# A two-layer encoder trunk on one core: two paddings resized, and the second half of the first activation block turned into a job of the first step

## The chip, the cores and the metric

The kernel runs on one core of one Trainium2 chip. The metric is the device time of one execution in microseconds. The kernel before was timed three times: 2141.28, 2142.65 and 2142.89 us, median 2142.65 us. A fourth execution was taken with the hardware profiler; its time was 2141.81 us.

## What is computed

The input x has 256 positions and 2048 features in float32. Two layers run one after the other, each a mixer followed by a SwiGLU feed-forward block, and a last RMSNorm ends the trunk. What matters here is the first matrix product, ab_in, which follows the first norm, and that every large product is a matmul of 128 x 128 by 128 x 512:

```
for layer in range(2):
    h = rms_norm(x, mix_norm[layer])
    x = x + (mixer_ab(h) if layer == 0 else mixer_c(h))
    h = rms_norm(x, ffn_norm[layer])
    x = x + (silu(h @ w_gate) * (h @ w_up)) @ w_down
out = rms_norm(x, final_norm)
```

## The kernel before, in words

**Products.** Each float32 product is made of three fp32r matmuls (function `three`, L480): the operands are split in a high part and a low rest (activations `xh`, `xl`; weights `whi`, `wlo`), and high x high (L481), high x low (L482) and low x high (L483) are added into one PSUM bank. The activations, transposed, are the stationary operand (loaded by a weight load); the weights are the moving operand of 512 columns. In the views a matmul is written `b<-moving,stationary`.

**Stages and steps.** Eight stages follow each other: ab_in (12 blocks of 512 output columns), ab_out (4), up0 (11), down0 (4), c_in (8), c_out (4), up1 (11), down1 (4). A block is cut into steps. A plain step (`kind` std) takes 4 of the 128-row pieces of the weights and makes 24 matmuls, 12 in each half; up0 and up1 are mixed stages whose steps combine operands to save products (24 or 21 matmuls a step, 183 a block; some take their moving operand from `ha` and `la` instead of `whi` and `wlo`). In all there are 376 steps and 8826 such matmuls.

**Operands.** The stationary operand is xh/xl in ab_in and c_in (pools x_a and x_next), cath/catl in ab_out (pool cat), ush/usl in c_out (pool us), fh/fl in the mixed stages (pool forms), jh/jl in down0 and down1 (pool split). Pools on the left side of SBUF are stacked in the order const, wpool, resid, small, and then the ones opened and closed during the work (x_a, mix_a, mixw, forms, x_next, split); cat, us, ffn and mix_c are stacked from the right side. Tiles take multiples of 32 bytes. Three tiles that nobody reads, CONST_PAD, SMALL_PAD and RIGHT_PAD, only shift what follows. In the program of the kernel before the bytes at which the tiles begin in a partition are:

```
stage .. mhalf (const)   16512, 17024, 17536, 17920, 18432   mhalf has 8 bytes
gain0 (const)            19392     = mhalf + 32 + 928
raw, whi, wlo (wpool)    19456 .. 68608                      all multiples of 1024
x0 .. x3 (resid)         76800 .. 89088                      all multiples of 1024
ssq (small)              93440     = 93184 + 256
xh0 (x_a), tt (mixw)     96320     = 94 x 1024 + 64
ha, la (mixw)            104512, 110656                      multiples of 1024 + 64
fh0, fl0, fh1, fl1       120896, 123968, 127040, 130112      multiples of 1024 + 64
fh2, fl2, fh3, fl3       133184, 136768, 140352, 143424      fl2 a multiple of 512 + 64
fh4, fl4 .. fh6, fl6     146496, 150080 .. 159808, 163392    fl4, fl6 likewise
jh, jl (split)           137280 .. 161856                    multiples of 1024 + 64
cath0 .. catl3, us       195584 .. 224256                    all multiples of 1024
```

**Order of work.** `load(t)` issues the weights of step t on SP's queue (three `raw` buffers), `prep(t)` splits them: two casts on ScalarE (L259, `whi`) and two subtractions on VectorE (L265, `wlo`), into one of two buffers, which is free when the step that used it is done. At the end of step t, `end_step` (L523) loads step t + 4 and prepares step t + 2. Other work is put in a heap by `later(dt, fn)` with a due time counted in half steps; `jobs_due(2t)` runs what is due at the beginning of step t and `jobs_due(2t + 1)` between its halves; equal due times keep the order in which they were put in. `x_transposes(st, n)` makes the operands xh and xl of 512 columns of x: per half 4 transposes on TensorE into a PSUM bank (banks 4 and 5 in turn, L127), two activations on ScalarE (L409), two operations on VectorE (L413). Until the job due at 9 the order on ScalarE and VectorE is that of the program (`manual_schedule`, L618 to L621, closed by L656); TensorE's order is chosen by the compiler's scheduler.

**The start.** On SP's queue, in order: columns 0 to 255 of x0 (the first 512 features of x), two pieces of the weights of step 0, columns 256 to 511 of x0, the rest of step 0's weights, x1, weights of step 1, x2, weights of step 2, x3, and later the weights of step 3. L642 to L657 then give the order of the preparation, which the change edits. The jobs put in are: x_transposes 2 due at 1, x_transposes 3 due at 3, squares of x0 to x3 due at 3 to 6, transpose_vectors due at 4, finish_norm due at 7.

Of the kernel before, what the change touches and what calls it, by code (L numbers as in the profile page):

```python
# [9 lines left out]
F32 = mybir.dt.float32  # L10
# [6 lines left out]
P = 128  # L17
# [17 lines left out]

CONST_PAD = 928
SMALL_PAD = 256
RIGHT_PAD = 992  # L40

RC = 4
# [3 lines left out]
PREP_AHEAD = 2  # L46
# [29 lines left out]
def trunk_kernel(  # L76
# [18 lines left out]
    nc = tc.nc  # L95

    const = ctx.enter_context(tc.tile_pool(name="const", bufs=1))
    wpool = ctx.enter_context(tc.tile_pool(name="wpool", bufs=1))
    resid = ctx.enter_context(tc.tile_pool(name="resid", bufs=1))
    small = ctx.enter_context(tc.tile_pool(name="small", bufs=2))  # L100
    small.tile([P, SMALL_PAD // 4], F32, name="small_pad", bufs=1)
    right = ctx.enter_context(tc.tile_pool(name="right", bufs=1, side="right"))
# [81 lines left out]
    def load(t):  # L184
        if t >= len(steps) or t in raws:
            return
        s = steps[t]
        r = wpool.tile([P, RC, NB], F32, tag="raw", name="raw", bufs=RAW_BUFS)
        raws[t] = r

        def part(dst, w, c0, k, n):
            nc.sync.dma_start(
                dst, w[k * P : (k + n) * P, c0 : c0 + NB].rearrange("(k p) n -> p k n", p=P)
            )

        if s.kind != "std":
            for side, (w, c0) in enumerate(s.src):
                part(r[:, side::2, :], w, c0, s.k0, 2)
            return
        (w, c0), = s.src  # L200
        if t:
            part(r, w, c0, s.k0, RC)
        else:
            for k in range(2):
                part(r[:, k : k + 1, :], w, c0, k, 1)
            return lambda: part(r[:, 2:4, :], w, c0, 2, 2)
# [5 lines left out]
    def prep_a_hi(t):  # L212

        if t in parts_a:
            return
        hi = mixw[0].tile([P, 3, NB], F32R, tag="ha", name="ha")
        nc.scalar.copy(hi, raws[t][:, 1:4, :])
        parts_a[t] = (hi, None)

    def prep_a_lo(t):  # L220
        hi, lo = parts_a[t]
        if lo is None:
            lo = mixw[0].tile([P, 3, NB], F32R, tag="la", name="la")
            nc.vector.tensor_tensor(
                out=lo, in0=raws[t][:, 1:4, :], in1=hi.bitcast(F32), op=ALU.subtract
            )
            parts_a[t] = (hi, lo)

    def combine_first(t):

        if t in sums:
            return
        load(t)
        sums[t] = tt = mixw[0].tile([P, RC, NB], F32, tag="tt", name="tt")
        r = raws[t]
        nc.vector.tensor_tensor(
            out=tt[:, 0:2, :], in0=r[:, 0:3:2, :], in1=r[:, 1::-1, :], op=ALU.subtract
        )

    def combine_rest(t):  # L240

        if t in whole:
            return
        combine_first(t)
        whole.add(t)
        r, tt = raws[t], sums[t]
        for i in range(2):
            nc.vector.tensor_tensor(
                out=tt[:, 2 + i, :], in0=r[:, 2 + i, :], in1=tt[:, 2 * i, :], op=ALU.subtract
            )  # L250

    def cast_half(t, h):
        if t not in parts:
            load(t)
            hi = wpool.tile([P, RC, NB], F32R, tag="whi", name="whi", bufs=W_BUFS)
            lo = wpool.tile([P, RC, NB], F32R, tag="wlo", name="wlo", bufs=W_BUFS)
            parts[t] = (hi, lo)
        r = sums[t] if steps[t].kind == "S" else raws[t]
        nc.scalar.copy(parts[t][0][:, HALF[h], :], r[:, HALF[h], :])  # L259

    def low_part(t, h):
        hi, lo = parts[t]
        r = sums[t] if steps[t].kind == "S" else raws[t]
        sl = HALF[h]
        nc.vector.tensor_tensor(  # L265
            out=lo[:, sl, :], in0=r[:, sl, :], in1=hi[:, sl, :].bitcast(F32), op=ALU.subtract
        )

    def prep(t):

        if t >= len(steps) or t in parts:
            return
        load(t)
        if steps[t].kind == "S":
            combine_first(t)
            combine_rest(t)
        for h in "01":
            cast_half(t, h)
            low_part(t, h)
        if steps[t].kind == "S":  # L280
            prep_a_hi(t)
            prep_a_lo(t)
        if steps[t].pi in operand:
            operand[steps[t].pi].split(steps[t].k0 // RC)
# [11 lines left out]
    def later(dt, fn):  # L296
        heapq.heappush(jobs, (now[0] + dt, seq[0], fn))
        seq[0] += 1
# [15 lines left out]
    ident = const.tile([P, P], F32, name="ident")  # L314
    make_identity(nc, ident)
    mhalf = const.tile([P, M], F32, name="mhalf")
    const.tile([P, CONST_PAD // 4], F32, name="const_pad")
    nc.gpsimd.memset(mhalf, -0.5)
    vec_at = {}
# [61 lines left out]
    def transpose_pair(src, c0):  # L381

        pt = tp_bank()
        for j in range(2):
            for m in range(M):
                nc.tensor.transpose(  # L386
                    out=pt[:, j * S + m * P : j * S + (m + 1) * P],
                    in_=src[:, m, c0 + j * P : c0 + (j + 1) * P],
                    identity=ident,
                )  # L390
        return pt
# [4 lines left out]
    def x_transposes(st, n, halves=(0, 1)):  # L396
        if st.mixed:
            for i in (2 * n, 2 * n + 1):
                x_forms(st, xs[n], i)
            return  # L400
        if n not in st.hi:
            st.hi[n] = st.pool[0].tile([P, 4, S], F32R, tag=f"xh{n}", name=f"xh{n}")
            st.lo[n] = st.pool[0].tile([P, 4, S], F32R, tag=f"xl{n}", name=f"xl{n}")
        hi, lo = st.hi[n], st.lo[n]
        for half in halves:
            pt = transpose_pair(xs[n], half * 2 * P)
            cols = [4 * n + half * 2 + j for j in range(2)]
            for j, c in enumerate(cols):
                nc.scalar.activation(  # L409
                    hi[:, c % 4, :], pt[:, j * S : (j + 1) * S], AF.Copy, scale=gain_col(st, c)  # L410
                )
            for j, c in enumerate(cols):
                nc.vector.scalar_tensor_tensor(  # L413
                    out=lo[:, c % 4, :], in0=pt[:, j * S : (j + 1) * S], scalar=gain_col(st, c),
                    in1=hi[:, c % 4, :].bitcast(F32), op0=ALU.mult, op1=ALU.subtract,
                )

    def x_forms(st, src, i):

        pt = tp_bank()  # L420
        c0 = (2 * i % 4) * P
        for j, (kk, m) in enumerate(((0, 1), (0, 0), (1, 0), (1, 1))):
            nc.tensor.transpose(  # L423
                out=pt[:, j * P : (j + 1) * P], in_=src[:, m, c0 + kk * P : c0 + (kk + 1) * P],
                identity=ident,
            )
        f = st.pool[0].tile([P, 8, P], F32, tag="f", name="f")
        for kk in range(2):
            nc.scalar.activation(
                f[:, 2 * kk : 2 * kk + 2, :].rearrange("p a b -> p (a b)"),  # L430
                pt[:, kk * S : (kk + 1) * S], AF.Copy, scale=gain_col(st, 2 * i + kk),
            )

        def combine(dst, a, b, op):
            nc.vector.tensor_tensor(out=f[:, dst, :], in0=f[:, a, :], in1=f[:, b, :], op=op)

        if MIX[i] == "S":
            combine(4, 0, 3, ALU.add)
            combine(5, 1, 0, ALU.subtract)
            combine(6, 4, 1, ALU.subtract)  # L440
            combine(7, 2, 6, ALU.subtract)
            n, used = S_FORMS, f[:, 1:8, :]
        else:
            combine(slice(4, 6), slice(1, 3), slice(0, 4, 3), ALU.subtract)
            n, used = N_FORMS, f[:, 0:6, :]
        hi = st.pool[0].tile([P, n, P], F32R, tag=f"fh{i}", name=f"fh{i}")
        lo = st.pool[0].tile([P, n, P], F32R, tag=f"fl{i}", name=f"fl{i}")
        split(hi, lo, used)
        st.hi[i], st.lo[i] = hi, lo
# [73 lines left out]
    def end_step(t, evac):  # L523
        now[0] = 2 * t + 2
        del parts[t]
        cur[0] += 1
        evac()
        load(t + LOAD_AHEAD)
        prep(t + PREP_AHEAD)

    BANKS = {1: 6, 6: 7, 7: 5, 2: 0, 5: 1, 3: 2, 4: 3}

# [90 lines left out]
    st = new_norm("mix0")  # L623
# [15 lines left out]
    def first_split(a, b):  # L639
        split(hi0[:, a:b, :], lo0[:, a:b, :], raws[0][:, a:b, :])  # L640

    x_transposes(st, 0, (0,))  # L642
    first_split(0, 1)
    first_split(1, 2)
    x_transposes(st, 0, (1,))
    first_split(2, 4)
    x_transposes(st, 1)
    parts[0] = (hi0, lo0)
    load(3)
    prep(1)  # L650
    for n in (2, 3):
        later(2 * n - 3, lambda n=n: x_transposes(st, n))
    for n in range(4):
# [504 lines left out]
```

## Time and profile before

| what | value |
|---|---|
| median of the three runs | 2142.65 us |
| the profiled execution | 2141.81 us, of which its span 2140.0 us |
| TensorE busy (matmul) | 2121.4 us, 99% of the span, 9356 instructions |
| VectorE busy | 1500.9 us, 70% |
| ScalarE busy | 1119.6 us, 52% |
| transfers | 404.80 MB, mean 189 GB/s |

The span runs from the first to the last instruction of the program; the rest of the execution's time lies around it. A busy TensorE is not TensorE at its peak: matmuls are pipelined, each is recorded from its start to its modelled end, and two of them overlap in the record. What a stream of matmuls costs is the time from one start to the next.

### The profile page before, as it was taken

How to read it: one execution, taken by the hardware profiler on the slowest of the kernel's cores; microseconds unless marked ns; L12 is line 12 of the kernel's file. 1: busy time of each engine (PE TensorE's matmuls, PEld its weight loads, DVE VectorE, ACT ScalarE, POOL GpSimd, SP SyncE). 2: the span in 40 equal slices, each digit the busy share in tenths (PEclk: the TensorE clock that was granted, in tenths of full speed). 3: DMA queues.
4: the chain of work that ended last, by engine and by line, in shares of the span. 5: the costliest groups of instructions: out<-in, count | busy, mean ns of one | idle time of the engine just before them, and what ended most of it. 6: DMA issues, size and time to landing. Idle time of an engine off the chain costs nothing.

```text
span 2140.0 us, 24018 instructions
## 1 busy us (share of the span) xinstructions
PE 2121.4 (99%) x9356; PEld 1715.4 (80%) x9356; DVE 1500.9 (70%) x1591; ACT 1119.6 (52%) x1327; POOL 17.8 (1%) x37
## 2 busy tenths in 40 slices
PE   8999999999999999999999999999999999999998
PEld 7888888888888888788888888888888888878886
DVE  4545556788888888766664465688888888866665
ACT  5444445555555555555554544555555555555554
POOL 1000000000000000000000000000000000000000
PEclk9999999999999999999999999999999999999999
DMA  7554555555555555555556555555555555655554
GB/s 249 176 181 163 181 190 180 189 203 177 196 197 197 191 197 183 190 184 182 192 186 231 185 175 172 183 200 183 196 188 201 197 180 194 212 187 187 191 183 137
DMA packets 205361, 404.80 MB, mean 189 GB/s; under 512 B 9436, under 2 KB 10048, under 8 KB 204992
## 3 DMA queue, kind: packets, MB, share of 16 engines
q1 hardware_dynamic: 203312, 397.45, 54.9%
q0 software_dynamic: 1328, 4.77, 0.7%
q8 instruction: 73, 1.20, 0.2%
q10 hardware_dynamic: 608, 1.06, 0.1%
q14 instruction: 40, 0.33, 0.0%
HBM read 401.14 MB, written 2.10 MB: 188 GB/s over the span
## 4 chain that ended last, share of the span: by engine, by line
PE 98%; DVE 1%; issue 0%; DMA 0%; ACT 0%; SPq 0%; POOLq 0%; POOL 0%; DVEq 0%
PE b L481 32%; PE b L482 32%; PE b L483 32%; PE b L386 2%; PE b L423 0%; PE b L1012 0%; DMA x<-in_x_dram 0%; DVE wlo L265 0%; PE b L702 0%; DVE sg L879 0%; PE b L746 0%; PE b L734 0%; PE b L749 0%; DVE j L210 0%; DVE hh L879 0%
## 5 line engine op out<-in xcount | busy, mean ns | idle before, releaser
L265 DVE TENSOR_TENSOR wlo<-raw,whi 128x1024 fp32r<-128x1024 f32 x618 | 728.9, 1221 | 291.1 <-ACT whi L259 290.8
L259 ACT CAST whi<-raw 128x1024 fp32r<-128x1024 f32 x618 | 617.5, 1048 | 447.0 <-PE b L483 321.0
L482 PE MATMUL b<-wlo,fh 128*128 128x512 f32 x1144 | 454.8, 398 | 0.0
L483 PE MATMUL b<-whi,fl 128*128 128x512 f32 x1144 | 451.3, 394 | 0.0
L481 PE MATMUL b<-whi,fh 128*128 128x512 f32 x1144 | 386.5, 396 | 0.0
L482 PE MATMUL b<-wlo,jh 128*128 128x512 f32 x688 | 272.3, 396 | 0.3 <-DVE wlo L265 0.3
L483 PE MATMUL b<-whi,jl 128*128 128x512 f32 x688 | 271.8, 395 | 0.0
L483 PEld LDWEIGHTS b<-whi,fl 128*128 128x128 f32 x1144 | 214.4, 187 | 50.7
L482 PE MATMUL b<-wlo,xh 128*128 128x512 f32 x640 | 254.9, 398 | 0.0
L482 PEld LDWEIGHTS b<-wlo,fh 128*128 128x128 f32 x1144 | 214.4, 187 | 50.5
L481 PEld LDWEIGHTS b<-whi,fh 128*128 128x128 f32 x1144 | 212.8, 187 | 51.9
L483 PE MATMUL b<-whi,xl 128*128 128x512 f32 x640 | 253.2, 396 | 0.0
L481 PE MATMUL b<-whi,jh 128*128 128x512 f32 x688 | 247.7, 396 | 0.0
L481 PE MATMUL b<-whi,xh 128*128 128x512 f32 x640 | 245.4, 402 | 0.0
L210 DVE TENSOR_TENSOR jl<-h,jh 128x1024 fp32r<-128x1024 f32 x86 | 105.2, 1225 | 157.3 <-ACT jh L209 154.8
L265 DVE TENSOR_TENSOR wlo<-tt,whi 128x1024 fp32r<-128x1024 f32 x132 | 157.2, 1221 | 65.5 <-ACT whi L259 65.5
L259 ACT CAST whi<-tt 128x1024 fp32r<-128x1024 f32 x132 | 134.4, 1050 | 127.2 <-PE b L483 102.4
L209 ACT CAST jh<-h 128x1024 fp32r<-128x1024 f32 x86 | 89.9, 1047 | 206.4 <-PE b L482 206.4
L482 PEld LDWEIGHTS b<-wlo,jh 128*128 128x128 f32 x688 | 129.3, 188 | 31.8 <-DVE wlo L265 0.7
L483 PEld LDWEIGHTS b<-whi,jl 128*128 128x128 f32 x688 | 129.3, 188 | 31.1
L481 PEld LDWEIGHTS b<-whi,jh 128*128 128x128 f32 x688 | 129.1, 188 | 30.8
L483 PEld LDWEIGHTS b<-whi,xl 128*128 128x128 f32 x640 | 120.4, 188 | 28.6
(157 smaller groups left out, 2091.9 us busy)
## 6 DMA issues: line engine op xcount, KB each, us to landing
raw<-in_ffn_w_gate_dram SPq DMA_DIRECT2D x176, 512.0 KB, 3.6
raw<-in_ffn_w_up_dram SPq DMA_DIRECT2D x176, 512.0 KB, 4.5
raw<-in_ffn_w_down_dram SPq DMA_DIRECT2D x88, 1024.0 KB, 4.9
raw<-in_ab_w_in_dram SPq DMA_DIRECT2D x47, 1024.0 KB, 4.9
raw<-in_c_w_in_dram SPq DMA_DIRECT2D x32, 1024.0 KB, 5.2
raw<-in_ab_w_out_dram SPq DMA_DIRECT2D x16, 1024.0 KB, 4.9
raw<-in_c_w_out_dram SPq DMA_DIRECT2D x16, 1024.0 KB, 4.9
x<-in_x_dram SPq DMA_DIRECT2D x3, 512.0 KB, 12.5
```

The lines of the kernel that those rows point to most:

```text
L209: nc.scalar.copy(hi, src)
L210: nc.vector.tensor_tensor(out=lo, in0=src, in1=hi.bitcast(F32), op=ALU.subtract)
L259: nc.scalar.copy(parts[t][0][:, HALF[h], :], r[:, HALF[h], :])
L265: nc.vector.tensor_tensor(out=lo[:, sl, :], in0=r[:, sl, :], in1=hi[:, sl, :].bitcast(F32), op=ALU.subtract)
L386: nc.tensor.transpose(out=pt[:, j * S + m * P : j * S + (m + 1) * P], in_=src[:, m, c0 + j * P : c0 + (j + 1) * P], identity=ident,)
L481: nc.tensor.matmul(ps, lhsT=ah, rhs=bh, start=start, stop=False)
L482: nc.tensor.matmul(ps, lhsT=ah, rhs=bl, start=False, stop=False)
L483: nc.tensor.matmul(ps, lhsT=al, rhs=bh, start=False, stop=stop)
```

## The change

Four things are edited. CONST_PAD becomes 896 and SMALL_PAD 192. A one-column tile `warm` is made in const, and ScalarE copies one column into it ahead of its other work. In the start, x_transposes of columns 256 to 511 of x0, the split of the second half of step 0's weights, `load(3)` and `prep(1)` become one job, `first_rest`, due at 1, and x_transposes 1 becomes a job due at 2. In `end_step`, after step 0, `prep(2)` is put in the heap with dt = 2 instead of being called; now[0] is 2 there.

```diff
-CONST_PAD = 928
-SMALL_PAD = 256
+CONST_PAD = 896
+SMALL_PAD = 192
...
     mhalf = const.tile([P, M], F32, name="mhalf")
+    warm = const.tile([P, 1], F32, name="warm")
     const.tile([P, CONST_PAD // 4], F32, name="const_pad")
...
         load(t + LOAD_AHEAD)
-        prep(t + PREP_AHEAD)
+        if t:
+            prep(t + PREP_AHEAD)
+        else:
+            later(2, lambda: prep(PREP_AHEAD))
...
+    nc.scalar.copy(warm, mhalf[:, 0:1])
     x_transposes(st, 0, (0,))
     first_split(0, 1)
     first_split(1, 2)
-    x_transposes(st, 0, (1,))
-    first_split(2, 4)
-    x_transposes(st, 1)
     parts[0] = (hi0, lo0)
-    load(3)
-    prep(1)
+
+    def first_rest():
+        x_transposes(st, 0, (1,))
+        first_split(2, 4)
+        load(3)
+        prep(1)
+
+    later(1, first_rest)
+    later(2, lambda: x_transposes(st, 1))
     for n in (2, 3):
         later(2 * n - 3, lambda n=n: x_transposes(st, n))
```

## Rows read from the trace of the kernel before

**Rows 1.** Page, part 4: the chain that ended last, share by engine.
```profile
PE 98%; DVE 1%; issue 0%; DMA 0%; ACT 0%; SPq 0%; POOLq 0%; POOL 0%; DVEq 0%
```

**Rows 2.** Instruction groups on TensorE: count | busy us, mean ns of one | idle before.
```profile
L482 PE MATMUL b<-wlo,fh 128*128 128x512 f32 x1144 | 454.8, 398 | 0.0
...
L482 PE MATMUL b<-wlo,jh 128*128 128x512 f32 x688 | 272.3, 396 | 0.3 <-DVE wlo L265 0.3
...
L482 PE MATMUL b<-wlo,xh 128*128 128x512 f32 x640 | 254.9, 398 | 0.0
...
L482 PE MATMUL b<-la,fh 128*128 128x512 f32 x198 | 77.3, 390 | 0.0
...
L482 PE MATMUL b<-wlo,cath 128*128 128x512 f32 x128 | 49.8, 389 | 0.0
```

**Rows 3.** Timeline of TensorE (start us, us of one): a stretch of c_in, one of c_out.
```profile
1280.04 0.39 PE L483 MATMUL b<-whi,xl 128*128 128x512 f32 x1
...
1287.74 0.39 PE L483 MATMUL b<-whi,xl 128*128 128x512 f32 x1
...
1345.19 0.39 PE L483 MATMUL b<-whi,usl 128*128 128x512 f32 x1
...
1350.63 0.39 PE L483 MATMUL b<-whi,usl 128*128 128x512 f32 x1
```

**Rows 4.** Stretches: us, busy us (count) of PE, PEld, DVE, ACT, POOL; PEclk, DMA.
```profile
9.30:12.00 2.70, 2.70 (x8) 2.15 (x7) 1.37 (x3) 1.77 (x3) 0.00 (x0) 1.00 1.06 359
...
45.20:53.40 8.20, 8.20 (x37) 6.58 (x36) 2.36 (x2) 2.00 (x2) 0.00 (x0) 1.00 0.54 165
...
502.00:545.51 43.51, 43.51 (x192) 35.03 (x192) 36.65 (x38) 22.89 (x24) 0.00 (x0) 1.00 0.56 194
...
1345.00:1361.00 16.00, 16.00 (x72) 13.27 (x71) 9.63 (x12) 9.16 (x13) 0.00 (x0) 1.00 0.58 197
```

**Rows 5.** Timeline of ScalarE at the start.
```profile
4.09 1.28 ACT L409 ACT_TABLE_LOAD   x1 [4.09 <-DVE gain L627]
...
14.13 1.74 ACT L409 ACTIVATE xh<-b,gain 128x256 fp32r<-128x256 f32 x4 [2.66 <-PE b L386]
15.77 1.99 ACT L259 CAST whi<-raw 128x1024 fp32r<-128x1024 f32 x2
17.81 1.75 ACT L409 ACTIVATE xh<-b,gain 128x256 fp32r<-128x256 f32 x4
...
25.93 0.63 ACT L360 ACTIVATE junk<-x 128x512 f32<-128x512 f32 x1
```

**Rows 6.** Timeline of VectorE at the start.
```profile
16.85 2.36 DVE L265 TENSOR_TENSOR wlo<-raw,whi 128x1024 fp32r<-128x1024 f32 x2
19.13 1.65 DVE L413 SCALAR_TENSOR_TENSOR xl<-b,gain,xh 128x256 fp32r<-128x256 f32 x4
```

**Rows 7.** Timeline of TensorE at the start; the line of 10.94 is from the chain.
```profile
3.94 1.11 PE L386 MATMUL b<-ident,x 128*128 128x128 f32 x4
...
9.32 1.20 PE L481 MATMUL b<-whi,xh 128*128 128x512 f32 x2
...
10.94 0.43 PE b L483
...
17.53 0.48 PE L481 MATMUL b<-whi,xh 128*128 128x512 f32 x1
...
24.01 0.48 PE L481 MATMUL b<-whi,xh 128*128 128x512 f32 x1
...
30.16 0.48 PE L481 MATMUL b<-whi,xh 128*128 128x512 f32 x1
```

**Rows 8.** Issues at 3.69 and at 12.76 us: weights of steps 1, 3, us to landing.
```profile
raw<-in_ab_w_in_dram SPq DMA_DIRECT2D x1, 1024.0 KB, 11.7
...
raw<-in_ab_w_in_dram SPq DMA_DIRECT2D x1, 1024.0 KB, 10.4
```

**Rows 9.** Timeline of TensorE at the end of up0.
```profile
870.60 0.40 PE L483 MATMUL b<-whi,fl 128*128 128x512 f32 x1
872.50 0.48 PE L481 MATMUL b<-whi,j 128*128 128x512 f32 x1 [1.51 <-DVE sg L879]
```

## The prediction

> **What bounds the kernel now.** I read the page's chain first: the work that ended last is 98% TensorE, nearly all on the three lines of `three` [rows 1]. So only two things can move the time: the interval from one 512-column matmul to the next, and TensorE's idle time. Idle time of over 1 us is found at the start and at the two ends of the mixed stages.
>
> The view of instruction groups splits the matmuls by their stationary operand [rows 2]. Each row stands for three lines with the same count: 3 x 1144 on fh/fl, 3 x 688 on jh/jl, 3 x 640 on xh/xl, and 3 x 198 with ha/la moving. With wlo moving, a matmul on fh, jh or xh is recorded at 396 to 398 ns, one on cath at 389; with la moving, one on fh takes 390. The timeline gives the interval between starts, which is what counts [rows 3]: on xl 7.70 us for 33 intervals, 233.3 ns; on usl 5.44 us for 24, 226.7 ns. The operand that moves, whi/wlo, is the same pool in both stages. The busy times of the other engines don't explain the 6.6 ns [rows 4]: in a stretch of ab_in with VectorE at 2.36 of 8.20 us and ScalarE at 2.00 the 37 matmuls are at the longer interval ((8.20 + 0.39) / 37 = 232), while c_out with VectorE at 9.63 of 16.00 us is at the shorter one ((16.00 + 0.39) / 72 = 228).
>
> What does differ is the address. cat and us lie at multiples of 1024 bytes, xh, xl, jh, jl, fh, fl, ha and la 64 bytes above a multiple of 512, and whi, wlo at multiples of 1024. la is off by 64 like fh, and its matmuls are short; so what counts seems to be how the two operands of a matmul stand to each other: 6.6 ns more where they are 64 bytes apart.
>
> **The paddings.** mhalf and the new warm take 32 bytes each, so CONST_PAD 896 leaves everything behind it in const where it was; wpool and resid don't move. SMALL_PAD 192 takes 64 bytes from small, so all pools on the left behind it move down by 64: xh0 from 96,320 to 96,256, which is 94 x 1024. All off-set operands land on multiples of 512, most on 1024, as cat and us do. The count: 1144 + 688 + 640 = 2472, times 3 = 7416 matmuls. The price of each is 6.6 ns by the starts, which are what adds up; by the two windows of [rows 4] it is 4. I take 6.2, near the starts, since they count 33 and 24 whole intervals and a window is out by up to one matmul: 46.0 us. The 594 with ha/la, short already with la, get 1.5 ns: 0.9 us. Gain **47 us**, 43 to 50 if the cause is right (5.7 to 6.6 ns, and the wait that VectorE may leave behind c_in's layer norm). VectorE isn't late next in the mixed stage: it works 36.65 of 43.51 us there [rows 4], and a block would become 42.4.
>
> Here a rule speaks against the change. The Trainium skill, "SBUF — State Buffer" (the box on cachelines under Door 1), gives SBUF lines of 16 bytes; and "TensorE: Matmul & The Clock Gate" (Part 2, step 1) says that TensorE reads weights and moving data through two ports, so that loading the next weights takes nothing from the running matmul. 64 bytes are four whole lines, so by these pages the offset is free and the 47 us would be 0; no row here shows a line size, and against the 0 stand the rows 2 and 3 above.
>
> **The start.** ScalarE and VectorE follow the program's order until the job due at 9 closes that order, so the order can be read from the code. Each step below is against [rows 5 to 7].
>
> The warm copy moves the activation table load (1.28 us, at 4.09) ahead of the data. xh0 could then start when its transposes end, near 5.1 (3.94 + 1.11), instead of when the load ends, at 5.4: 0.3 us. It costs a one-column copy in idle time.
>
> Half 0 of step 0 is now issued ahead of the second transposes, so TensorE can begin when the first cast is done, near 6.5 instead of 9.32; it runs at half rate there (0.43 us each, as 512 columns take at the 1.2 GHz level, though the granted clock of that window reads 1.00 [rows 4]). That would be worth up to 2.5 us if the rest could follow. It can't, in three places:
>
> (a) Step 1. Before, ScalarE makes xh1 (14.13), then whi1 (15.77), then xh2 (17.81), and step 1 starts at 17.53. After, due 1 brings first_rest with whi1, then x_transposes 2; x_transposes 1 is due at 2, behind both. The weights of step 1 are issued at 3.69 and land 11.7 us later, at 15.4 [rows 8], so whi1 runs 15.45 to 17.45, xh2 to 19.1. xh1 also needs its PSUM bank, which xl2 frees: VectorE does wlo1 (2.36 us from 16.55) and xl2 (0.84 a pair) to 19.75; transposes to 20.25, xh1's first pair to 21.15. Step 1 starts near 21.2, 3.7 us late (20.0 if the bank doesn't bind).
>
> (b) Step 2. end_step(0) now puts prep(2) at due 4, the beginning of step 2; but end_step(1) runs prep(3) before that. So on ScalarE and VectorE the weights of step 2 are queued behind those of step 3, which land at 12.76 + 10.4 = 23.2, and behind squares (two of 0.63 us and their reads, some 1.5 us for an x tile). They go into the buffer of step 1, free only when step 1 ends. ScalarE after xh1 (22.0): xh3 to 24.3, squares to 25.8, whi3 to 27.75, squares to 29.3, whi2's first half to 30.3; wlo2's first half ends at 31.5. Matmuls into one bank keep their order, so two can start and the third waits for wlo2: 31.5 + 22 x 0.23 = 36.6 for the end of step 2, where step 3 started at 30.16. If the transposes of xh3 stand behind half of step 1 on TensorE, all is 2 us later. So the start **loses 6.4 to 8.4 us**; I take 7.4. SP is not late: the weights of steps 3 and 4 wait on the DMA queue anyway.
>
> (c) The clock. TensorE would idle twice for some 3 us, with transposes between. An idle of 1.9 us (870.6 to 872.5) is followed by full rate [rows 9]. Longer ones aren't shown: from nothing to a second slow start for each (the eight matmuls of 9.30 to 12.00 at 0.43 instead of 0.23: 1.6 us), so 0 to 3.2; I take 0.6, nearer to the row.
>
> Were prep(4) to wait for the buffer of step 3, 2 us more. Start in all: 8 us lost, from 2 (waits covered better than I read) to 13.
>
> **Sum.** The profiled execution took 2141.81 us (span 2140.0), 0.84 below the median of the runs, 2142.65. 2141.81 - 47 + 8 = 2102.8; against the median, **2103.6**. Within this case 2142.65 - 50 + 2 = 2094.7 to 2142.65 - 43 + 13 = 2112.7.
>
> **Rivals.**
> - *The offset isn't the cause* and the start decides. cat and us also differ by lying above byte 195,584, farther from whi than all others. Then the paddings give 0 and the swapped weights of steps 2 and 3 on ScalarE cost their 8 us: 2150.7, slower. For it: only two stages show the short interval, and both lie there. Against it: the matmuls of la on fh lie low in the partition and are short too. It decides from where the paddings give under 8 us, that is under 1.1 of the 6.2 ns. The two pages named above give this time. Chance 0.09.
> - *The start gains.* If the order leaves TensorE fed, it starts 2.5 us earlier and nothing is lost: 2142.65 - 47 - 2.5 = 2093.2. Against it: the landing at 15.4 and the order of prep. Chance 0.09.
> - *The paddings do only half.* fl2, fl4 and fl6 (3584-byte tiles before them) land on 512, not 1024, so the change doesn't do what it says for them; or VectorE, at 84% in the mixed stage, holds its blocks. Then the 4026 matmuls there bring nothing: 47 - 0.9 - 3432 x 6.2 ns = 25: 2142.65 - 25 + 8 = 2125.7. Chance 0.06.
> - My forecast: 0.76.
>
> **How the numbers follow.** The range takes my case and the start's gain, 2092 to 2113, and leaves out the half case and the slower one, 0.15. A measurement of this kernel tells about 0.2% (4.3 us) from no change. Faster: 0.76 + 0.09 + 0.06 = 0.91. Of the slower rival 0.03 stays within 0.2% (a start that loses under 4.3 us), 0.06 is slower.
>
> **What would show it.** The interval on xl, jl and fl at 227 instead of 233 ns; if it stays at 233 the paddings did nothing, whatever the total. On ScalarE, xh2 before xh1, and the third pair of whi casts waiting near 23 us; first matmuls of steps 1, 2 and 3 near 21, 30 and 36.6 us instead of 17.53, 24.01 and 30.16. If step 3 starts before 30, my order of the start is wrong. A TensorE idle inside the mixed blocks would mean that VectorE is the next bound.

## The result, and the profile after

The changed kernel takes 2107.69 us (median of four, 2105.94 to 2109.13) against 2142.7 (2141.28 to 2142.89): a ratio of 0.9838, 95% interval 0.9821 to 0.9855. It is faster by 35 us (1.6%), 4.1 us slower than forecast and inside the range. The profiled execution took 2108.35 us, its span 2106.5. Lines have moved: the three matmuls of `three` are L482 to L484, transposes L387, xh L410, xl L414, squares L361.

From the page of the changed kernel, busy time by engine and the shares of the chain that ended last:

```profile
PE 2080.0 (99%) x9356; PEld 1720.2 (82%) x9356; DVE 1500.3 (71%) x1591; ACT 1121.4 (53%) x1328; POOL 17.8 (1%) x37
...
PE 96%; DVE 1%; ACT 1%; issue 1%; DMA 1%; SPq 0%; POOLq 0%; POOL 0%; DVEq 0%; ACTq 0%
```

As many matmuls as before, and TensorE still ends last; but ACT, issue and DMA now have 1% of the chain each, where [rows 1] rounds them to 0. So there are two questions: how fast the stream runs, and what the new 1% are.

The stream. The groups that answer to [rows 2], in the changed kernel:

```profile
L483 PE MATMUL b<-wlo,fh 128*128 128x512 f32 x1144 | 449.3, 393 | 0.0
...
L483 PE MATMUL b<-wlo,jh 128*128 128x512 f32 x688 | 268.0, 390 | 0.4 <-DVE wlo L265 0.4
...
L483 PE MATMUL b<-wlo,xh 128*128 128x512 f32 x640 | 253.4, 396 | 0.2 <-DVE wlo L265 0.2
...
L483 PE MATMUL b<-la,fh 128*128 128x512 f32 x198 | 77.0, 389 | 0.0
```

fh went from 398 to 393 ns and jh from 396 to 390. The xh group shows 396 because it holds the slow matmuls of the start; the timeline is the cleaner reading. TensorE in c_in, the answer to the first pair of [rows 3]:

```profile
1265.55 0.39 PE L484 MATMUL b<-whi,xl 128*128 128x512 f32 x1
...
1273.03 0.39 PE L484 MATMUL b<-whi,xl 128*128 128x512 f32 x1
```

Again 33 intervals: 7.48 us, 226.7 ns each, where it was 233.3. That is the interval that c_out had all along.

The start. ScalarE in the changed kernel (start us, us of all):

```profile
1.22 1.28 ACT L646 ACT_TABLE_LOAD   x1 [1.22 <-PEq L1153]
...
15.46 2.00 ACT L259 CAST whi<-raw 128x1024 fp32r<-128x1024 f32 x2 [4.71 <-DMA raw<-in_ab_w_in_dram]
17.52 1.57 ACT L410 ACTIVATE xh<-b,gain 128x256 fp32r<-128x256 f32 x4
20.46 0.84 ACT L410 ACTIVATE xh<-b,gain 128x256 fp32r<-128x256 f32 x2 [1.37 <-PE b L387]
21.62 0.84 ACT L410 ACTIVATE xh<-b,gain 128x256 fp32r<-128x256 f32 x2 [0.33 <-PE b L387]
26.08 0.84 ACT L410 ACTIVATE xh<-b,gain 128x256 fp32r<-128x256 f32 x2 [3.62 <-PE b L387]
28.82 0.84 ACT L410 ACTIVATE xh<-b,gain 128x256 fp32r<-128x256 f32 x2 [1.90 <-PE b L387]
...
30.93 1.97 ACT L259 CAST whi<-raw 128x1024 fp32r<-128x1024 f32 x2
...
34.19 1.97 ACT L259 CAST whi<-raw 128x1024 fp32r<-128x1024 f32 x2
```

By the order of the program the casts at 15.46, 30.93 and 34.19 are whi of steps 1, 3 and 2, and the activations at 17.52 make xh2, those at 20.46 and 21.62 xh1, those at 26.08 and 28.82 xh3. VectorE makes xl2 at

```profile
18.82 1.65 DVE L414 SCALAR_TENSOR_TENSOR xl<-b,gain,xh 128x256 fp32r<-128x256 f32 x4
```

and TensorE has:

```profile
7.84 1.08 PE L387 MATMUL b<-ident,x 128*128 128x128 f32 x4 [2.68 <-DMA x<-in_x_dram]
8.58 1.20 PE L482 MATMUL b<-whi,xh 128*128 128x512 f32 x2
...
19.79 0.63 PE L387 MATMUL b<-ident,x 128*128 128x128 f32 x4 [1.87 <-issue]
20.62 0.97 PE L387 MATMUL b<-ident,x 128*128 128x128 f32 x4 [0.20 <-DVE xl L414]
21.23 0.77 PE L482 MATMUL b<-whi,xh 128*128 128x512 f32 x1
...
25.44 0.60 PE L387 MATMUL b<-ident,x 128*128 128x128 f32 x4
...
28.18 0.60 PE L387 MATMUL b<-ident,x 128*128 128x128 f32 x4
...
35.27 1.22 PE L482 MATMUL b<-whi,xh 128*128 128x512 f32 x2 [5.94 <-ACT whi L259]
...
43.84 0.39 PE L482 MATMUL b<-whi,xh 128*128 128x512 f32 x1
```

The rows of 21.23, 35.27 and 43.84 are the first matmuls of steps 1, 2 and 3 (counted: 24 large matmuls a step); before they stood at 17.53, 24.01 and 30.16 [rows 7], and the forecast was 21, 30 and 36.6. Step 3 is 13.68 us late. Two numbers close the account: from step 3 to the end the kernel before needs 2140.02 - 30.16 = 2109.86 us, the changed one 2106.55 - 43.84 = 2062.71, **47.15 less**; 13.68 - 47.15 = -33.47, which is the difference of the spans.

By stages, from the first matmul of one to that of the next (the last row ends at the last large matmul):

| stage | before, us | after, us | difference | large matmuls |
|---|---|---|---|---|
| ab_in from step 3 | 271.40 | 265.03 | -6.37 | 1080 |
| ab_out | 90.73 | 90.68 | -0.05 | 384 |
| up0 | 480.21 | 468.88 | -11.33 | 2013 |
| down0 | 249.97 | 243.09 | -6.88 | 1056 |
| c_in | 190.50 | 186.16 | -4.34 | 768 |
| c_out | 90.71 | 90.68 | -0.03 | 384 |
| up1 | 480.21 | 468.88 | -11.33 | 2013 |
| down1 | 247.64 | 240.82 | -6.82 | 1056 |

What was off by 64 bytes gains 5.6 to 6.5 ns a matmul, waits and the matmuls with ha or la included; what wasn't (ab_out, c_out) gains nothing.

### The profile page after: what moved, and what is told of

It reads as the page before. It is cut to its first block, busy times and chain, and to the rows that moved or that the text cites. A ratio compares the mean times of both kernels' runs of the same rounds, so it can differ in the third digit from the quotient of the medians.

```text
span 2106.5 us, 24018 instructions
## 1 busy us (share of the span) xinstructions
PE 2080.0 (99%) x9356; PEld 1720.2 (82%) x9356; DVE 1500.3 (71%) x1591; ACT 1121.4 (53%) x1328; POOL 17.8 (1%) x37
## 4 chain that ended last, share of the span: by engine, by line
PE 96%; DVE 1%; ACT 1%; issue 1%; DMA 1%; SPq 0%; POOLq 0%; POOL 0%; DVEq 0%; ACTq 0%
PE b L482 31%; PE b L483 31%; PE b L484 31%; PE b L387 2%; DMA raw<-in_ab_w_in_dram 1%; DVE wlo L265 1%; ACT whi L259 0%; PE b L424 0%; PE b L711 0%; PE b L1021 0%; ACT junk L988 0%; DVE vt L1008 0%; DVE sg L888 0%; PE b L755 0%; DVE vt L1009 0%
## 5 line engine op out<-in xcount | busy, mean ns | idle before, releaser
L483 PE MATMUL b<-wlo,fh 128*128 128x512 f32 x1144 | 449.3, 393 | 0.0
L484 PE MATMUL b<-whi,fl 128*128 128x512 f32 x1144 | 445.4, 389 | 0.0
L482 PE MATMUL b<-whi,fh 128*128 128x512 f32 x1144 | 380.6, 391 | 0.0
L483 PE MATMUL b<-wlo,jh 128*128 128x512 f32 x688 | 268.0, 390 | 0.4 <-DVE wlo L265 0.4
L484 PE MATMUL b<-whi,jl 128*128 128x512 f32 x688 | 267.3, 389 | 0.0
L484 PE MATMUL b<-whi,xl 128*128 128x512 f32 x640 | 251.6, 394 | 0.0
L482 PE MATMUL b<-whi,xh 128*128 128x512 f32 x640 | 245.1, 400 | 5.9 <-ACT whi L259 5.9
L484 PEld LDWEIGHTS b<-whi,fl 128*128 128x128 f32 x1144 | 214.9, 188 | 43.6
L482 PEld LDWEIGHTS b<-whi,fh 128*128 128x128 f32 x1144 | 213.2, 188 | 45.0
L482 PE MATMUL b<-whi,jh 128*128 128x512 f32 x688 | 242.9, 389 | 0.0
L484 PEld LDWEIGHTS b<-whi,jl 128*128 128x128 f32 x688 | 129.1, 188 | 26.7
L482 PEld LDWEIGHTS b<-whi,jh 128*128 128x128 f32 x688 | 128.9, 188 | 26.7
L482 PEld LDWEIGHTS b<-whi,xh 128*128 128x128 f32 x640 | 122.0, 191 | 30.9 <-ACT whi L259 6.3
## 6 DMA issues: line engine op xcount, KB each, us to landing
x<-in_x_dram SPq DMA_DIRECT2D x3, 512.0 KB, 12.5
```

The lines of the kernel that those rows point to most:

```text
L482: nc.tensor.matmul(ps, lhsT=ah, rhs=bh, start=start, stop=False)
L483: nc.tensor.matmul(ps, lhsT=ah, rhs=bl, start=False, stop=False)
L484: nc.tensor.matmul(ps, lhsT=al, rhs=bh, start=False, stop=stop)
```

## The experiments

### The two halves apart

One kernel is the kernel before with the padding of small alone; CONST_PAD stays 928, as there is no new tile in const:

```diff
-SMALL_PAD = 256
+SMALL_PAD = 192
```

> The kernel before with SMALL_PAD 192 and nothing else. Theory (the offset sets the matmul interval): the interval on xl, jl and fl falls from 233 to 227 ns and the time by the 47.2 us that the changed kernel gained between its step 3 and its end, 2142.7 - 47.2 = 2095.5 us. Rival (the gain of the changed kernel came with its other start, or with the scheduler's other order): the interval stays at 233 and the time at 2142.7.

Measured: 2094.96 us (2094.49 to 2095.34), before 2142.42; ratio 0.9777 [0.9763, 0.9792]. The other is the changed kernel with the old padding, which puts the operands back at +64:

```diff
-SMALL_PAD = 192
+SMALL_PAD = 256
```

> The changed kernel with SMALL_PAD 256, so that the operands stand where they stood before. Theory: the start alone costs what step 3 began later, 13.7 us: 2142.7 + 13.7 = 2156.4 us, with the interval at 233 ns. Rival (what looks like the start's loss is made up later, or comes from the paddings): 2142.7 within 3 us.

Measured: 2154.96 us (2153.68 to 2155.38), ratio 1.0056 [1.0039, 1.0072]. TensorE in c_in, first with the padding alone (33 intervals), then with the start alone (27):

```profile
1252.59 0.39 PE L483 MATMUL b<-whi,xl 128*128 128x512 f32 x1
...
1260.07 0.39 PE L483 MATMUL b<-whi,xl 128*128 128x512 f32 x1
```

```profile
1293.54 0.39 PE L484 MATMUL b<-whi,xl 128*128 128x512 f32 x1
...
1299.84 0.39 PE L484 MATMUL b<-whi,xl 128*128 128x512 f32 x1
```

7.48 / 33 = 226.7 ns and 6.30 / 27 = 233.3 ns. The interval goes with the padding and with nothing else in the change. The halves add: -47.46 and +12.54 make -34.92, and the whole change has -35.0. What follows is that the new start loses some 12.6 us and that the kernel before with one number changed beats the changed kernel.

### Which property of the address

cat and us differ from the other operands in two ways: they are multiples of 1024, and they lie above byte 195,584. This kernel shifts the weights up by 64 and leaves the x, forms and split operands at +64, so that nothing in ab_in, c_in and the mixed and down stages is a multiple of 1024, but the distance of the two operands is one; now cat and us are 64 below the weights:

```diff
-CONST_PAD = 928
-SMALL_PAD = 256
+CONST_PAD = 992
+SMALL_PAD = 192
```

> The kernel before with SMALL_PAD 192 and CONST_PAD 992: xh, xl, jh, jl, fh, fl, ha and la stay where they were (64 above a multiple of 512), whi and wlo move up by 64 as well, cath, catl, ush and usl stay at multiples of 1024. Theory (the distance between the moving and the stationary operand counts): xl, jl and fl fall to 227 ns although their own address is unchanged, and the 768 matmuls on cat and us rise to 233; the time is 2142.7 - 46 + 4.7 = about 2101 us. Rival one (each operand's own address counts): all are at 233 or more, cat and us included or at most half way, 2142.7 or above. Rival two (cat and us are fast because they lie high in the partition): cat and us stay at 227, the others at 233.

Measured: 2096.7 us (one run). TensorE in c_in (33 intervals), and in c_out (15):

```profile
1252.79 0.39 PE L483 MATMUL b<-whi,xl 128*128 128x512 f32 x1
...
1260.30 0.39 PE L483 MATMUL b<-whi,xl 128*128 128x512 f32 x1
...
1321.52 0.39 PE L483 MATMUL b<-whi,usl 128*128 128x512 f32 x1
...
1324.96 0.39 PE L483 MATMUL b<-whi,usl 128*128 128x512 f32 x1
```

xl: 7.51 / 33 = 227.6 ns (mean over c_in 227.1), short although no operand is a multiple of 1024. usl: 3.44 / 15 = 229.3 ns (mean over c_out 229.0), longer than the 226.7 of [rows 3], in the place in SBUF where it was short. So it is the distance between the two operands, and the place alone does nothing. But a distance of -64 costs some 2.1 ns here (229.0 for 226.9), and not the 6.6 of +64 that my theory gave it. Either the sign counts, or these two stages feel a distance less than the others do: no run has +64 in ab_out and c_out, or -64 elsewhere, so that is open. 768 matmuls by 2.1 ns are 1.6 us, and in the traces ab_out and c_out are 0.8 us longer each than with the paddings alone (91.47 and 91.48 us, there 90.68).

The next four are the kernel before with other values of SMALL_PAD, so that the operands of ab_in, c_in, the mixed and the down stages stand 32, 128, 256 and 512 bytes above a multiple of 512 or 1024:

```diff
-SMALL_PAD = 256
+SMALL_PAD = 224
```

(224 stands for 32 bytes, 320 for 128, 448 for 256 and 704 for 512.)

> The kernel before with SMALL_PAD 224: xh, xl, jh, jl, fh, fl, ha and la stand 32 bytes above multiples of 512, whi and wlo at multiples of 1024. If any distance that is no multiple of 512 costs the 6 ns: interval near 233, time near 2142. If only some low bit of the distance counts (64, or all below 128): either 227 and 2095 or 233 and 2142.

> The kernel before with SMALL_PAD 320: the same operands 128 bytes above multiples of 512. If what counts is any distance off 512: 233 and 2142 us; if the pattern repeats every 128 bytes or less: 227 and 2095 us.

> The kernel before with SMALL_PAD 448: the same operands 256 bytes above multiples of 512. If what counts is any distance off 512: 233 and 2142 us; if the pattern repeats every 256 bytes or less: 227 and 2095 us.

> The kernel before with SMALL_PAD 704: the same operands 512 bytes above multiples of 1024. The stationary slices of 512 bytes then still begin at multiples of 512 as half of those on cat and us do today: 227 and 2095 us by the theory. Rival (the 1024 of the change's title counts): 233 and 2142 us, or between.

One run each; the kernel before took 2143.23 us beside them. The group of wlo on jh at 32, 128, 256 and 512 bytes, count | busy, mean ns of one:

```profile
L482 PE MATMUL b<-wlo,jh 128*128 128x512 f32 x688 | 272.8, 396 | 0.3 <-DVE wlo L265 0.3
```

```profile
L482 PE MATMUL b<-wlo,jh 128*128 128x512 f32 x688 | 271.7, 395 | 0.3 <-DVE wlo L265 0.3
```

```profile
L482 PE MATMUL b<-wlo,jh 128*128 128x512 f32 x688 | 267.9, 389 | 0.4 <-DVE wlo L265 0.4
```

```profile
L482 PE MATMUL b<-wlo,jh 128*128 128x512 f32 x688 | 268.3, 390 | 0.4 <-DVE wlo L265 0.4
```

| bytes from weights to activations | interval in c_in, ns (mean of all under 260 ns) | time, us |
|---|---|---|
| 0 (padding alone) | 227.0 | 2094.96 |
| 32 | 233.3 | 2141.08 |
| 64 (before) | 233.3 | 2142.65 |
| 128 | 232.5 | 2137.09 |
| 256 | 227.0 | 2094.43 |
| 512 | 227.0 | 2095.21 |

At 256 and 512 the cost is gone: a multiple of 256 is as good as the multiples of 1024 of the change, so fl2, fl4 and fl6, which land on multiples of 512, lose nothing by it. 32 costs as much as 64, and 128 0.8 ns less; that much over 7416 matmuls is 5.9 us, and the run has 6.1 less than the kernel before beside it (5.5 by the traces, from step 3 to the end).

### Where the start loses

Three kernels undo parts of the new order of the start and keep everything else. In the first, `prep(2)` is called at the end of step 0 again:

```diff
-        if t:
-            prep(t + PREP_AHEAD)
-        else:
-            later(2, lambda: prep(PREP_AHEAD))
+        prep(t + PREP_AHEAD)
```

> The changed kernel with prep of step 2 called at the end of step 0, as before the change. Theory (step 2 waits because its casts are queued behind those of step 3): the idle of 5.9 us ahead of step 2 goes, with the slow matmuls behind it; but the casts of step 2 now stand ahead of xh1 on ScalarE and their data lands at 19.3, so step 1 starts some 2 us later, near 23.2. Step 3 starts near 37 instead of 43.8, the time is about 2101 us. Rival (step 2 waits for something else, the transposes of x3 or the buffer): step 2 still starts at 35 and the time stays at 2107.7.

Measured: 2099.84 us (one run). On ScalarE:

```profile
19.66 2.00 ACT L259 CAST whi<-raw 128x1024 fp32r<-128x1024 f32 x2 [0.32 <-DMA raw<-in_ab_w_in_dram]
```

and on TensorE, step 1's last wait and the first matmul of step 2:

```profile
22.08 0.79 PE L482 MATMUL b<-whi,xh 128*128 128x512 f32 x1 [0.34 <-ACT xh L410]
...
29.72 0.40 PE L482 MATMUL b<-whi,xh 128*128 128x512 f32 x1
```

The weights of step 2 are cast at 19.66, when they land, instead of at 34.19, and step 2 follows step 1 with no wait. Step 1 pays 0.85 us (22.08 for 21.23), as its xh now stand behind that cast. Step 3 starts at 35.33 instead of 43.84. In the time this one edit is worth 7.9 us of the 12.7 between the changed kernel and the paddings alone.

In the second, x_transposes 1 is due at 1 instead of 2, ahead of x_transposes 2:

```diff
-    later(2, lambda: x_transposes(st, 1))
+    later(1, lambda: x_transposes(st, 1))
```

> The changed kernel with x_transposes 1 due at 1, ahead of x_transposes 2. Theory (step 1 waits for xh1, which stands behind xh2 on ScalarE and for its bank behind xl2 on VectorE): step 1 starts near 18.4 instead of 21.2. Step 2 still waits for casts queued behind those of step 3, near 32 to 34 instead of 35.3, so most of the 2.8 us is lost again there; time 2105 to 2107 us. Rival (step 1 waits for its weights or for TensorE's order): step 1 still starts at 21.

Measured: 2105.56 us (one run), 2.1 less than the changed kernel; its four runs spread over 3.2 us, so the time alone doesn't show a gain, and the trace has to. TensorE, first matmuls of steps 1 and 2:

```profile
17.89 0.50 PE L482 MATMUL b<-whi,xh 128*128 128x512 f32 x1 [0.25 <-ACT xh L410]
...
33.25 1.22 PE L482 MATMUL b<-whi,xh 128*128 128x512 f32 x2 [5.53 <-ACT whi L259]
```

Step 1 is back at 17.89, 3.3 us earlier than 21.23, and step 2 still waits for whi of step 2: it starts 2.0 us earlier (33.25 for 35.27). The two losses are in series, and only 2 us of the 3.3 come out behind the second wait.

The third has both edits.

> The changed kernel with both moves undone: x_transposes 1 due at 1 and prep of step 2 called at the end of step 0. Theory (these two orders and the slow matmuls that follow them are the whole of the start's 13.7 us): step 1 starts near 18.4, step 3 near 31, time 2095 to 2096.5 us, the paddings alone. Rival (first_rest itself or the half step in which it is issued costs too): 2098 or more.

Measured: 2097.39 us (one run), between the two theories: 10.3 of the 12.7 us are back. ScalarE in this kernel:

```profile
24.51 0.84 ACT L410 ACTIVATE xh<-b,gain 128x256 fp32r<-128x256 f32 x2 [1.92 <-PE b L387]
25.23 1.99 ACT L259 CAST whi<-raw 128x1024 fp32r<-128x1024 f32 x2
```

and in the one with the paddings alone:

```profile
18.68 1.75 ACT L409 ACTIVATE xh<-b,gain 128x256 fp32r<-128x256 f32 x4
20.31 2.00 ACT L259 CAST whi<-raw 128x1024 fp32r<-128x1024 f32 x2
```

In both the cast of step 2's weights stands behind xh2. With both edits xh2 waits for its transposes, which stand at 21.11 and 23.87 among step 1's matmuls, and at 18.04 and 18.95 with the paddings alone; why the scheduler put them later isn't shown. The cast comes 4.9 us later, and step 2 starts at 26.33 instead of 24.76: 1.6 of the 2.4 us that remain.

### The clock

The kernel before has 5 matmuls some 0.43 us apart at its start; the one with the paddings alone 10, the changed kernel 25 (11 in step 0, 5 in step 1, 9 in step 2). Against the usual 0.23 that is 0.20 us each. The 5 and the 10 are no sign of the padding: the seven kernels that keep the old start (before, the paddings alone, left by 64, and 32 to 512 bytes) have the same order on TensorE there, and from 3 (left by 64) and 4 (256 bytes) to 10 such matmuls; their step 3 starts from 29.73 to 30.90 us. So about 1 us of such a start belongs to the execution and not to the kernel; against the paddings alone (30.81) step 3 of the changed kernel is 13.0 us late, and not 13.68. Stretches of the changed kernel (columns as in [rows 4]):

```profile
8.50:13.80 5.30, 5.30 (x15) 4.19 (x14) 2.10 (x3) 1.77 (x3) 0.00 (x0) 1.00 1.04 388
21.20:24.00 2.80, 2.80 (x9) 2.21 (x8) 1.75 (x4) 0.93 (x3) 0.00 (x0) 0.50 0.94 360
35.20:41.00 5.80, 5.70 (x13) 4.01 (x14) 2.36 (x2) 2.31 (x6) 0.00 (x0) 0.50 0.91 290
```

The granted clock reads 0.50, the 1.2 GHz level, in steps 1 and 2, after TensorE had done nothing but transposes from 16.8 to 21.2 us and nothing from 29.3 to 35.27. The Trainium skill, "TensorE: Matmul & The Clock Gate" (Part 1), says that idle time takes the array to half its clock. The row of 35.20 agrees; ahead of the row of 21.20 TensorE wasn't idle throughout, as 16 transposes ran there.

To price it, one kernel is the paddings alone with 12 matmuls that nobody reads in the idle time ahead of the first large one; they add work and take none out:

```diff
     x_transposes(st, 0, (0,))
+    busy = ms_bank()
+    for _ in range(12):
+        nc.tensor.matmul(busy[:, 0:P], lhsT=ident, rhs=ident, start=True, stop=True)
```

> The paddings alone, with 12 matmuls of ident on ident (128 columns) into an unused bank between the first transposes and the second, in TensorE's idle time at the start; the result is not used. Theory (the first matmuls run at the 1.2 GHz level because TensorE idled from 5.0 to 8.5): fewer of the first matmuls take 0.43 us, step 3 starts up to 1.5 us earlier, 2093.5 to 2095 us. Rival (the slow matmuls at the start cover work that others do in that time): fewer slow matmuls, but step 1 waits for whi1 all the same and the time stays at 2095.

Measured: 2094.41 us (2094.19 to 2094.84), ratio 0.9779 [0.9763, 0.9796]. TensorE at the start of it:

```profile
4.96 5.15 PE L645 MATMUL b<-ident 128*128 128x128 f32 x24
...
10.30 0.71 PE L481 MATMUL b<-whi,xh 128*128 128x512 f32 x2
10.85 0.39 PE L482 MATMUL b<-wlo,xh 128*128 128x512 f32 x1
11.08 0.39 PE L483 MATMUL b<-whi,xl 128*128 128x512 f32 x1
```

The 12 are recorded as 24. No slow matmul is left (10.85 to 11.08 is 0.23). But the added ones also push the first large one from 9.12 to 10.30. Step 3 starts at 29.56, 1.25 us earlier than in the one trace of the paddings alone (30.81), as the theory has it, yet hardly earlier than in the kernel with 256 bytes (29.73), which has 4 slow matmuls and none added. The time is 0.6 us below the paddings alone, and the ranges of the two overlap: a gain isn't shown.

The other is the changed kernel with such matmuls in both waits:

```diff
+    def busy_1():
+        ps = ms_bank()
+        for _ in range(20):
+            nc.tensor.matmul(
+                ps[:, 0:P], lhsT=ident, rhs=raws[1][:, 0, 0:P], start=True, stop=True
+            )
+
+    def busy_2():
+        ps = ms_bank()
+        for _ in range(23):
+            nc.tensor.matmul(
+                ps, lhsT=st.hi[3][:, 3, 0:P], rhs=st.hi[0][:, 0:2, :], start=True, stop=True
+            )
+
+    later(2, busy_1)
     later(2, lambda: x_transposes(st, 1))
+    later(4, busy_2)
```

> The changed kernel with matmuls whose results are not used in TensorE's two idle times: 20 of 128 columns ahead of step 1 and 23 of 512 columns behind step 1. They shorten no wait. Theory (the idle times make TensorE fall to the 1.2 GHz level, and the slow matmuls of steps 1 and 2 are part of the 13.7 us): the 17 slow matmuls of steps 1 and 2 go, 3 to 3.5 us are saved, about 2104.5 us. Rival (the slow ones only fill time in which the casts would be waited for): no slow ones, but 2107 or more.

Measured: 2106.01 us (2105.41 to 2107.26), ratio 0.9834 [0.9819, 0.9848]. Its stretches:

```profile
21.20:24.00 2.80, 2.67 (x14) 2.03 (x13) 1.66 (x4) 1.57 (x4) 0.00 (x0) 1.00 0.76 218
35.20:41.00 5.80, 5.27 (x24) 4.30 (x24) 1.70 (x2) 1.60 (x5) 0.00 (x0) 1.00 0.97 329
```

The clock stays at 1.00, the 2.4 GHz level, 24 matmuls instead of 13 fit in the second stretch, and step 3 starts at 40.94 instead of 43.84, though step 1 starts 0.6 us later behind the added matmuls (21.83 for 21.23): the clock cost the start 2.9 us. (In the kernel with the start alone, which has the changed kernel's order, step 3 starts at 43.74.) The profiled executions agree (2105.55 and 2108.35 us), the medians differ by 1.7, and the intervals of the two ratios overlap; so the 2.9 us are shown in the traces, and the time by itself doesn't show a gain.

## Why the prediction was right, and which terms were mis-sized

**The paddings: right.** Forecast 47 us, measured 47.15 from step 3 to the end and 47.46 by the paddings alone. The 6.2 ns lie within the 5.6 to 6.5 of the stages. The mixed stages didn't meet VectorE: 468.88 / 11 = 42.6 us a block, forecast 42.4. The first rival, that the offset is not the cause, is dead by three runs: the interval follows the padding (226.7 with the paddings alone, 233.3 with the start alone), and the left-by-64 kernel has xl short at its old address and usl 2.1 ns longer at its own. So is the rival of half the paddings: up0 and up1 gave 11.33 us each. Two things were weaker than the total looks. I drew the distance from la on fh, short at 390 ns; ha on fh and ha on fl stand at the same +64 and were recorded at 394 and 393, so that row alone didn't carry the conclusion, and that it held is in part luck. And the 1.5 ns for the 594 matmuls with ha or la came from no row: these three groups now take 390, 389 and 389 ns, some 3 ns less each, so about 1.8 us where I took 0.9.

By the rule that I set against the change (the Trainium skill, "SBUF — State Buffer", cachelines, and "TensorE: Matmul & The Clock Gate", Part 2, on the two ports) 32 and 64 bytes are whole lines and would be free. The 233.3 ns at 32 and at 64 against 227.0 at 0 and 256 say otherwise, and the measurement decides.

**The start, step 1: right, and for its reason.** Forecast 21.2, measured 21.23; whi1 at 15.46 (forecast 15.45), and xh2 at 17.52 stands ahead of xh1 at 20.46. The bank binds too: the first transposes of x1 start at 19.79, 0.1 us after VectorE is done with xl2's first pair (19.69), though the view puts their wait down to "issue", and the last ones at 20.62 wait for xl, as the bank's owner. The run with x_transposes 1 ahead of x_transposes 2 undoes the loss (17.89).

**The start, step 2: right cause, too small.** `prep(2)` did stand behind `prep(3)` and the squares, and the run with `prep(2)` called directly shows it. What was off is the place of x3's transposes. I priced them at 0 or, behind half of step 1, at 2 us, and took the middle. They run at 25.44, behind half of step 1, and at 28.18, behind 22 of its 24 matmuls, so xh3 is done at 29.66 and not at 24.3. From there everything has nearly the forecast spacing (squares 1.4, whi3 1.9, squares 1.4), and whi2 starts at 34.19 instead of 29.3: 4.9 us. Some 4.3 of these are the order, since with the clock kept up step 3 still starts 4.3 us behind the 36.6 that I had worked out (40.94). Taken 1, measured 4.3.

**The clock: mis-sized.** Bounded by 0 and 3.2, taken 0.6 "nearer to the row" [rows 9], measured 2.9. That row is an idle of 1.5 us alone (the 1.9 of the prediction counts from start to start); here the waits were 4.8 us with transposes in them and 6 us. The upper bound would have been the better reading: the nearest row was not near.

Together: 4.3 - 1 + 2.9 - 0.6 = 5.6, and the start lost 13.68 in the trace where I took 8. That is outside the 2 to 13 that I gave the start; by the times of the two halves it is 12.5 to 12.7, just inside. The time missed by less, 4.1 us, since the profiled execution of before stands 0.84 us below its median and that of the changed kernel 0.66 above: that part is luck.

**Smaller steps.** The early start of TensorE (6.5 us) didn't come: the scheduler kept the second transposes ahead of the first large matmul (7.84, then 8.58). By the prediction it would have brought nothing; no run shows it. The table load moved to 1.22 and is off the path. `prep(4)` didn't add to it: its cast at 44.04 came with step 3 just begun, and no wait follows.

## What to carry to other kernels

Where matmuls with a stationary and a moving operand from SBUF follow each other at the bound, look at the distance of their addresses modulo 256 bytes, and spend a dummy tile to make it 0: one constant was worth 2.2% here (fp32r operands, 128 x 128 by 128 x 512, a new weight load for each matmul). Apart from that, a job moved on an in-order engine is late by whatever was queued ahead of it, and each wait that results may also cost the clock behind it. When two parts of a change pull in opposite directions, time each alone: the best version here is the kernel before with SMALL_PAD 192 (2094.96 us), 12.7 us below the whole change; SMALL_PAD 448 and 704 are as good (2094.43 and 2095.21, one run each), and the 12 unread matmuls (2094.41) add nothing that can be told apart.

## What the runs showed of the hardware that I hadn't expected

- +32 and +64 bytes cost some 6.3 ns a matmul, +128 5.5, and 256 and 512 nothing; -64 cost about 2.1, in other stages. No other distances were tried, and no run here tells which of the two reads, the weight load or the moving operand, is held up: the mean weight load is 188 ns at either interval.
- A matmul can be longer though its own two operands stand at the same offset. ha and fl are both at +64 in the kernel before and in the left-by-64 kernel, at the same addresses; of what TensorE reads in these stages only whi and wlo have moved. The group of ha on fl, first before, then left by 64:

```profile
L483 PE MATMUL b<-ha,fl 128*128 128x512 f32 x198 | 77.7, 393 | 0.0
```

```profile
L483 PE MATMUL b<-ha,fl 128*128 128x512 f32 x198 | 77.0, 389 | 0.0
```

  So these 4 ns seem to come with the weights, the operands of the neighbouring matmuls in the stream; how is open.
- The granted clock does not show every slow stretch. In 8.50:13.80 of the changed kernel it reads 1.00 while 15 matmuls are counted in 5.30 us. The trace's record of the clock begins only at 13.93 us there (at 12.17 in the kernel before, behind the stretch 9.30:12.00 of [rows 4]), and a stretch without a record is shown as 1.00; the spacing of the starts, 0.43 us, is the reading to trust.
